# Twelve input projection groups per layer as seven products of quarters, with the mix kept in DRAM, in a two-layer hybrid decoder trunk

## The chip, the cores and the metric

One NeuronCore of one Trainium2 chip runs the whole program. The metric is the device time of one execution in microseconds (us); lower is better. A core has TensorE (PE; its weight loads are PEld), VectorE (DVE), ScalarE (ACT), GpSimd (POOL) and SyncE (SP), which here only issues DMAs. Each works through its own instructions in the order in which the program was built.

## What is computed

Two layers. Each normalises its input, multiplies it by one wide input matrix, runs three head groups on the product (short convolution, stick-breaking attention, gated linear attention or GLA), multiplies each by a SiLU gate, and sends the 2048 mixed columns through an output matrix into the residual stream. Cut to what matters:

```python
D_MODEL = 2048; SEQ = 512; DEPTH = 2
h = _rmsnorm(x, norm_g)
proj = h @ w_in                         # 512 x 2048 times 2048 x 7696
(cv_h, cv_b, cv_c, cv_g, sb_q, sb_k, sb_v, sb_g, gl_q, gl_k, gl_v, gl_g, gl_lr) = split(proj)
y_conv = cv_b * (conv3(cv_c * cv_h) + conv_b) * silu(cv_g)                 # 512 columns
y_sb   = stick_breaking(rms(sb_q), rms(sb_k), sb_v) * silu(sb_g)           # 8 heads of 128
g      = log_sigmoid(gl_lr @ gla_w_up + gla_b_up) / 16
y_gla  = rms(gla(gl_q, gl_k, gl_v, g)) * silu(gl_g)                        # 4 heads, 512 columns
x      = x + concat([y_conv, y_sb, y_gla]) @ w_out
```

## The kernel before

Everything is float32 at the interface. Each factor of a large product is held as two float16 parts, high and low, and a product is three matmuls: high by high, high by low, low by high.

**Groups.** The columns of both matrices are worked off in groups of 256 (`specs`, lines 301 to 316): per layer 30 groups of `w_in` in the order gla v 0, v 1 (with 16 more columns, `gl_lr`), q, k, gate 0, gate 1, conv h, c, g, b of the first half, then four times (j = 0 to 3) v, g, q, k of two attention heads, then conv h, c, g, b of the second half; then 8 groups of `w_out`. A group is a step of a pipeline. `fetch(i+2)` (line 332) issues two DMAs of 1 MB on SP's queue into one of two `st` buffers. `load(i+1)` (line 423) makes the float16 parts: ACT squares and sums both halves for a bound (`wmax`, line 352), POOL sums over the partitions (line 362), DVE makes a scale (lines 363 to 379), ACT writes the high halves (`whi`, line 415, 128x2048 each) and DVE the low halves (`wlo`, line 421). The parts go into three pairs of buffers `wh`, `wl`, of which a plain group uses two. The call to `weights()` (line 467) at the start of group i starts `fetch(i+2)` and `load(i+1)` with a higher priority than the rest.

**Products on PE.** `project_cols` (line 611) makes 96 matmuls of 512 moving columns (lines 623 to 625), the result transposed; `project_toks` (line 635) and `project_by_token` (line 730) make 192 of 256 (lines 631 to 633, and 738). `project_quick` (line 686) forms the product from seven products of quarters instead of eight, and is used for the output groups in `QUICK` (line 30): three in layer 0 and four in layer 1. It makes 336 matmuls of 128 columns (line 698). It needs sums of quarters of both factors. Those of the weights are made in `wsums` (line 436): four DVE additions in place on the `st` buffer (lines 456, 458, 459, 462) and seven splits of 128x1024, each one ACT copy (line 450) and one DVE subtraction (line 451). They fill all three `wh`, `wl` pairs and a fourth pair, taken from `e` and `ga`. Those of the mix are made in `msums` (line 648), once a layer: 24 DVE operations (line 655) and 8 ACT copies (line 665), all 128x1024. Between the products ACT and DVE read the two PSUM banks of the group (lines 709 to 727), and a product that writes a bank waits for the reader of that bank (product 3 for the ACT copy at line 709, product 4 for the DVE subtraction at line 711).

**Around them.** GLA is in lines 912 to 1028: for each of two pairs of heads, seven levels of DVE, ACT and PE work, then a normalisation. It is emitted after the GLA gates, and its instructions lie beside the groups conv h 0 to v 0. Its float16 scratch (`src16`, `tgt16`, `att16`, lines 770 to 776) lies in the part of the mix buffers that the attention heads fill later. The attention of pair j (lines 1104 to 1165) is cut in four pieces that run beside the groups of the next pair (`go`, line 1100). For q and k of a pair the product is copied out of PSUM (line 1198), normalised in a chain of small DVE operations (line 1205 and lines 1207 to 1214), split (lines 1218, 1219) and transposed by DMA.

**The mix** is two SBUF tensors `mh`, `ml` of 128x4x16x128 float16. `mixsplit` (line 787) writes one block of 128 columns of it, on ACT and DVE; `weight_ratio` (line 1030) brings all blocks to one scale before the output groups.

**Order of the work.** The first 50 us or so of ACT and DVE are written out by hand (lines 553 to 604). Everything else is put into each engine's order by a scheduler when the program is built, by priority and by its own estimate of when an instruction is ready; at run time each engine keeps that order.

Of the kernel before, what the change touches and what calls it, by code (L numbers as in the profile page):

```python
# [17 lines left out]
P = 128  # L18
EPS = 1e-6
TAU = 16.0  # L20
XBITS = 8.0
# [8 lines left out]
QUICK = ((3, 4, 6), (3, 4, 5, 6))  # L30

AHEAD = (8, 17, 21)


# [5 lines left out]
def hybrid_trunk(ctx, tc, x, norm_g, w_in, conv_w, conv_b, sb_qn_g, sb_kn_g,  # L40
# [16 lines left out]
    big = ctx.enter_context(tc.tile_pool(name="big", bufs=4))  # L57
# [13 lines left out]
    def sm(n, tag, bufs=None):  # L71
        return small.tile([P, n], F32, tag=tag, name=nm(tag), bufs=bufs)
# [4 lines left out]
    def newbig(tag, shape, dt):  # L77
        return big.tile(shape, dt, tag="big", name=nm(tag))
# [12 lines left out]
    xt = [newbig("x", [P, 2, D], F32) for _ in range(2)]  # L91
# [210 lines left out]
    specs = []  # L302
    for l in range(depth):
        for cols in ([(GL_V, GW)], [(GL_V + GW, GW), (GL_LR, LR)], [(GL_Q, GW)], [(GL_K, GW)],
                     [(GL_G, GW)], [(GL_G + GW, GW)]):
            specs.append((l, w_in, cols))
        conv = [[(l, w_in, [(c0 + j * GW, GW)]) for c0 in (CV_H, CV_C, CV_G, CV_B)] for j in range(2)]
        specs += conv[0]
        for j in range(4):
            for c0 in (SB_V, SB_G, SB_Q, SB_K):  # L310
                specs.append((l, w_in, [(c0 + j * GW, GW)]))
        specs += conv[1]
        for gi in range(NG):
            if gi in QUICK[l]:
                quick.add(len(specs))
            specs.append((l, w_out, [(gi * GW, GW)]))
# [8 lines left out]
    staged, whole, peak, scales = {}, {}, {}, {}  # L325
# [6 lines left out]
    def fetch(i):  # L332

        l, src, cols = specs[i]
        staged[i] = st = []
        whole[i] = stage.tile([P, KT, GX], F32, tag="st", name=nm("st"))
        for h in range(2):
            s_ = whole[i][:, h * HK:(h + 1) * HK, :]
            o = 0
            for c0, w in cols:  # L340
                nc.sync.dma_start(
                    s_[:, :, o:o + w],
                    src[l, h * HK * P:(h + 1) * HK * P, c0:c0 + w].rearrange("(k p) n -> p k n", p=P))
                o += w
            st.append(s_)

    def wmax(i, h):

        n = sum(c[1] for c in specs[i][2])
        if h == 0:  # L350
            peak[i] = sm(2, "wm")
        S.activation(junk(HK * n).rearrange("p (k n) -> p k n", k=HK), staged[i][h][:, :, :n], AF.Square,  # L352
                     accum_out=peak[i][:, h:h + 1])

    def wscale(i):
# [4 lines left out]
        if i:  # L360
            gm = sm(2, "wgm")
            G.partition_all_reduce(gm, peak.pop(i), P, RED.add)  # L362
            V.tensor_scalar(m, gm[:, 0:1], gm[:, 1:2], 2.0 ** -120, ALU.add, ALU.max)  # L363
# [47 lines left out]
    def whi(i, h):  # L411
        n = sum(c[1] for c in specs[i][2])
        wh = wpool.tile([P, HK, GX], F16, tag="wh", name=nm("wh"))
        wl = wpool.tile([P, HK, GX], F16, tag="wl", name=nm("wl"))
        lasthi[i] = S.activation(wh[:, :, :n], staged[i][h][:, :, :n], AF.Copy, scale=scales[i])  # L415
        loaded[i][0].append((wh, wl))

    def wlo(i, h):
        n = sum(c[1] for c in specs[i][2])
        wh, wl = loaded[i][0][h]  # L420
        V.scalar_tensor_tensor(wl[:, :, :n], staged[i][h][:, :, :n], scales[i], wh[:, :, :n], ALU.mult, ALU.subtract)  # L421
# [14 lines left out]
    def wsums(i):  # L436
# [7 lines left out]
        parts.append([wk([P, HK * P], t, dt=F16) for t in ("e", "ga")])  # L444
# [99 lines left out]
    def halves(tag):  # L544

        return [newbig(tag, [P, NT, KT, P], F16) for _ in range(2)]

    mix = halves("x")
# [58 lines left out]
    for l in range(depth):  # L607
# [40 lines left out]
        def msums():  # L648

            parts = [[wk([P, 2, HK, P], tag, bufs, F16) for _ in range(2)] for tag, bufs in  # L650
                     (("zw", None), ("v", None), ("th", 2))]
            parts.append([wk([P, 2, HK, P], tag, 1, F16) for tag in ("raw", "qp")])
# [4 lines left out]
            if last:  # L657
                room = [a[:, n] for a in [newbig("x", [P, 4, HK, P], F32) for _ in range(2)] for n in range(3)]
            for t in range(2):
                (h11, h12), (h21, h22), (l11, l12), (l21, l22) = (  # L660
                    (a[:, q, 0::2, :], a[:, q, 1::2, :]) for a in mix for q in (t, t + 2))
# [6 lines left out]
                if last:  # L668
                    e, g, f = room[3 * t:3 * t + 3]
                else:  # L670
                    e, g, f = (wk([P, HK, P], tag) for tag in ("g", "g", "kT"))
# [14 lines left out]
        def project_quick(sums):  # L686
# [4 lines left out]
            a11, a12, a22 = ([a[:, 2 * r:2 * r + 2, c::2, :] for a in mix] for r, c in ((0, 0), (0, 1), (1, 1)))  # L691
            s_, a21_22, a12_s, a11_21 = sums

            def prod(o, w, a, start, stop=False):
                for t in range(2):
                    for kk in range(HK):
                        for i, (p_, q_) in enumerate(((0, 0), (0, 1), (1, 0))):
                            T.matmul(o[:, t * P:(t + 1) * P], a[p_][:, t, kk, :], w[q_][:, kk, :],  # L698
                                     start=start and t == kk == i == 0, stop=stop and kk == HK - 1 and i == 2,
                                     skip_group_check=True)  # L700

            def half(a, r, c):
                return y[:, 2 * r:2 * r + 2, c * P:(c + 1) * P], a.rearrange("p (t c) -> p t c", c=P)

            y = wk([P, NT, GW], "g")
            tmp = wk([P, 4, GW], "g")
            p1, v_, d7, u_ = (tmp[:, n, :] for n in range(4))
# [8 lines left out]
            o, a = half(pa, 0, 0)  # L716
            S.activation(o, a, AF.Copy)
            prod(pb, wt1, a21_22, False, True)
            V.tensor_tensor(u_, pb, p1, ALU.subtract)
            o, a = half(pf, 0, 1)  # L720
            V.tensor_tensor(o, a, half(u_, 0, 1)[1], ALU.add)
            o, a = half(u_, 1, 1)
            V.tensor_tensor(o, a, half(d7, 1, 1)[1], ALU.subtract)
            yield 0, y[:, :2, :].rearrange("p a c -> p (a c)"), u
            prod(pd, wT4, a22, False, True)
            o, a = half(pd, 1, 0)
            V.tensor_tensor(o, a, half(v_, 1, 0)[1], ALU.subtract)
            yield 2, y[:, 2:, :].rearrange("p a c -> p (a c)"), u
# [14 lines left out]
        def gate(ps, u, mx=None, logistic=False):  # L743

            g = wk([P, 2, seq], "g")
            for c in range(2):
                y = g[:, c, :]
                if logistic:
                    tables.append(S.activation(y, ps[c], AF.Sigmoid, scale=u))
                    for a in tables[-9:-1]:  # L750
                        order(tables[-1], a)
                    V.scalar_tensor_tensor(y, ps[c], u, y, ALU.mult, ALU.mult)
# [9 lines left out]
            if mx is not None:  # L762
                V.tensor_reduce(mx, g, AX.XY, ALU.max, apply_absolute_value=True)
            return g

        mix = halves("m")
        mh, ml = mix


        spare = [[mh[:, t, 4:12, :].rearrange("p k c -> p (k c)")[:, n * seq:(n + 1) * seq] for n in range(2)]  # L770
                 for t in range(NT)]
# [539 lines left out]
```

## Time and profile before

| what | value |
|---|---|
| time, median of three runs | 1719.39 us (1718.61 to 1720.03) |
| time of the profiled execution | 1721.89 us |
| span of that execution, first instruction to last | 1720.1 us |
| granted TensorE clock, mean | 0.997 |
| HBM read, written | 173.36 MB, 8.39 MB |

Times within the trace count from the start of the span. A row of the groups view has the source line, the engine, the operation, what it writes and reads, the shape, the count, the busy time, the mean length of one in ns, and the idle time of the engine before it with what ended it. A row of the windows view has for each engine the busy time in that stretch and the instruction count, then the granted clock and the busy share of the DMA engines.

### The profile page before, as it was taken

What the parts mean: (1) busy time and instruction counts of PE and PEld (TensorE: products, weight loads), DVE (VectorE), ACT (ScalarE), POOL (GpSimd) and SP (SyncE); (2) the same over time, 40 slices, a digit from 0 to 9 for tenths busy, and PEclk for the clock granted to TensorE, in tenths of its full rate; (3) what the DMA queues carried; (4) which work ended last, traced back from release to release, by engine and by line L of the source; (5) the groups of instructions that cost most, each with busy time, mean ns of one, the idle gap of its engine ahead of it and who ended that gap; (6) DMA issues with size and microseconds to landing.
All of it is one profiled execution on the core that took longest, in us unless ns stands there. A gap on an engine that the chain in (4) does not pass through costs nothing. (4 is left out here: it accounts for less than half of the span.)

```text
span 1720.1 us, 32415 instructions
## 1 busy us (share of the span) xinstructions
PE 1702.0 (99%) x13770; PEld 1227.2 (71%) x13770; DVE 1166.7 (68%) x2149; ACT 1022.4 (59%) x1243; POOL 63.5 (4%) x104
## 2 busy tenths in 40 slices
PE   7999999999999999999999999999999999999998
PEld 5744557878787764799986454668686868548998
DVE  8566897566666656786675588974656566567883
ACT  7558676555555555566655575864555555545661
POOL 1100000000000000000010000000000000000000
PEclk9999999999999999999999999999999999999999
DMA  7323321344444445145544231223544433343441
GB/s 251 98 98 98 99 98 54 113 120 126 119 121 123 129 123 153 61 156 181 181 116 148 83 108 55 99 98 111 126 127 126 125 108 108 116 137 123 148 155 45
DMA packets 266641, 204.95 MB, mean 119 GB/s; under 512 B 93362, under 2 KB 265724, under 8 KB 265984
## 3 DMA queue, kind: packets, MB, share of 16 engines
q1 hardware_dynamic: 257488, 193.42, 37.1%
q10 hardware_dynamic: 9008, 9.45, 1.6%
q8 instruction: 108, 1.77, 0.4%
q14 instruction: 37, 0.30, 0.1%
HBM read 173.36 MB, written 8.39 MB: 106 GB/s over the span
## 5 line engine op out<-in xcount | busy, mean ns | idle before, releaser
L421 DVE SCALAR_TENSOR_TENSOR wl<-st,ws,wh 128x2048 f16<-128x2048 f32 (+1 forms) x138 | 324.4, 2352 | 205.3 <-ACT wh L415 205.3
L415 ACT ACTIVATE wh<-st,ws 128x2048 f16<-128x2048 f32 (+1 forms) x136 | 272.0, 2003 | 247.0 <-PE psp L633 111.0
L633 PE MATMUL psp<-wh,m 128*128 128x256 f16 x1216 | 331.5, 273 | 0.0
L632 PE MATMUL psp<-wl,m 128*128 128x256 f16 x1216 | 331.4, 273 | 0.0
L631 PE MATMUL psp<-wh,m 128*128 128x256 f16 x1216 | 331.4, 273 | 0.0
L352 ACT ACTIVATE junk<-st 128x2048 uint8<-128x2048 f32 (+1 forms) x150 | 285.5, 1903 | 4.9 <-DMA st<-in_w_out_dram 3.0
L633 PE MATMUL psp<-wh,x 128*128 128x256 f16 x768 | 209.3, 273 | 0.0
L632 PE MATMUL psp<-wl,x 128*128 128x256 f16 x768 | 209.3, 273 | 0.0
L631 PE MATMUL psp<-wh,x 128*128 128x256 f16 x768 | 209.3, 273 | 0.0
L623 PE MATMUL psp<-m,wh 128*128 128x512 f16 x512 | 194.0, 379 | 0.0
L624 PE MATMUL psp<-x,wh 128*128 128x512 f16 x512 | 194.0, 379 | 0.0
L624 PE MATMUL psp<-m,wh 128*128 128x512 f16 x512 | 194.0, 379 | 0.0
L623 PE MATMUL psp<-x,wh 128*128 128x512 f16 x512 | 194.0, 379 | 0.0
L625 PE MATMUL psp<-x,wl 128*128 128x512 f16 x512 | 193.9, 379 | 0.0
L625 PE MATMUL psp<-m,wl 128*128 128x512 f16 x512 | 193.9, 379 | 0.0
L625 PEld LDWEIGHTS <-wl 128*128 128x128 f16 x1024 | 100.2, 98 | 119.7
L624 PEld LDWEIGHTS <-wh 128*128 128x128 f16 x1024 | 100.2, 98 | 118.7 <-issue 2.6
L623 PEld LDWEIGHTS <-wh 128*128 128x128 f16 x1024 | 100.2, 98 | 117.5 <-issue 1.9
L631 PEld LDWEIGHTS <-m 128*128 128x128 f16 x1216 | 119.0, 98 | 13.9
L633 PEld LDWEIGHTS <-m 128*128 128x128 f16 x1216 | 119.0, 98 | 13.9
L632 PEld LDWEIGHTS <-m 128*128 128x128 f16 x1216 | 119.0, 98 | 13.8
L363 DVE TENSOR_SCALAR wq<-wgm 128x1 f32<-128x1 f32 x75 | 15.9, 212 | 111.1 <-POOL wgm L362 111.1
(356 smaller groups left out, 2665.0 us busy)
## 6 DMA issues: line engine op xcount, KB each, us to landing
st<-in_w_in_dram SPq DMA_DIRECT2D x120, 1024.0 KB, 7.7
st<-in_w_out_dram SPq DMA_DIRECT2D x32, 1024.0 KB, 7.6
x<-in_x_dram SPq DMA_DIRECT2D x4, 1024.0 KB, 5.1
qT<-in_x_dram ACTq DMA_DIRECT2D x8, 512.0 KB, 6.4
qT<-xs ACTq DMA_DIRECT2D x8, 512.0 KB, 3.9
xs<-x SPq DMA_DIRECT2D x14, 256.0 KB, 3.8
out_dram<-kT SPq DMA_DIRECT2D x14, 256.0 KB, 2.1
th<-za SPq DMA_TRANSPOSE x64, 3.1
```

Source lines behind the costliest of these rows:

```text
L352: S.activation(junk(HK * n).rearrange("p (k n) -> p k n", k=HK), staged[i][h][:, :, :n], AF.Square, accum_out=peak[i][:, h:h + 1])
L363: V.tensor_scalar(m, gm[:, 0:1], gm[:, 1:2], 2.0 ** -120, ALU.add, ALU.max)
L415: lasthi[i] = S.activation(wh[:, :, :n], staged[i][h][:, :, :n], AF.Copy, scale=scales[i])
L421: V.scalar_tensor_tensor(wl[:, :, :n], staged[i][h][:, :, :n], scales[i], wh[:, :, :n], ALU.mult, ALU.subtract)
L623: T.matmul(o, wh[:, kk, cs], xh[:, :, k, :], start=st_, stop=False)
L624: T.matmul(o, wh[:, kk, cs], xl[:, :, k, :], start=False, stop=False)
L625: T.matmul(o, wl[:, kk, cs], xh[:, :, k, :], start=False, stop=en)
L631: T.matmul(o, ah[:, t, k, :], wh[:, kk, :n], start=st_, stop=False, skip_group_check=True)
L632: T.matmul(o, ah[:, t, k, :], wl[:, kk, :n], start=False, stop=False, skip_group_check=True)
L633: T.matmul(o, al[:, t, k, :], wh[:, kk, :n], start=False, stop=en, skip_group_check=True)
```

## The change

- Twelve `w_in` groups of each layer (`QUICK_IN`) go through `project_quick`: both GLA gates, conv h, c, g of the first half, v of pairs 1 and 3, g of all four pairs, and conv h of the second half. All but the two v groups give a transposed result; there `project_quick` makes 168 matmuls of 256 columns, for the v groups 336 of 128.
- The sums of quarters of the input are made once a layer (`xsums`), after the decay of GLA is known in the program's text, by the code that makes those of the mix.
- The result of a quick group is put together in an SBUF tile of its own (`dst`) that is taken when the group starts; a plain group is still read from PSUM.
- The large buffers stay four of 128x16 KB, but two on each of two sides. The sums of the input lie where the mix was. So `mixsplit` writes to a `ga` tile and a DMA on SP's queue stores it in DRAM (`mixd`); after conv h of the second half `mixload` reads what is there back in six DMAs, and the last four blocks are written to SBUF as before.
- The scratch of GLA lies in the attention buffers `qp` and `th`.
- The `st` buffer is 256 columns wide; the 16 columns of `gl_lr` have a tile and a DMA of their own. The fourth pair of weight buffers has tiles of its own. Most small tiles have one buffer in place of two. One power of two in the scale of x changes.

The parts of the diff that the text speaks of:

```diff
+QUICK_IN = ("gla gate 0", "gla gate 1", "conv h 0", "conv c 0", "conv g 0", "v 1", "g 0", "g 1", "g 2", "v 3", "g 3",
+            "conv h 1")
...
-        parts.append([wk([P, HK * P], t, dt=F16) for t in ("e", "ga")])
+        parts.append([wk([P, HK * P], t, 1, dt=F16) for t in ("w7h", "w7l")])
...
+        def xsums():
+
+            parts = []
+            for _ in range(2):
+                a = newbig("s", [P, 4, 2, HK, P], F16, 1 - l)
+                parts.extend([a[:, 2 * n], a[:, 2 * n + 1]] for n in range(2))
+            return sums_of((xh, xl), parts, lambda t: [wk([P, HK, P], tag) for tag in ("zw", "zw", "g")])
...
-        def project_quick(sums):
+        def project_quick(src, sums, y, cols):
...
+                            if cols:
+                                T.matmul(o, w[q_][:, kk, :], a[p_][:, :, kk, :], start=st_, stop=en,
+                                         skip_group_check=True)
+                            else:
+                                T.matmul(o[:, t * P:(t + 1) * P], a[p_][:, t, kk, :], w[q_][:, kk, :], start=st_,
+                                         stop=en, skip_group_check=True)
...
             prod(pa, w11, a11, True)
-            S.activation(p1, pa, AF.Copy)
+            S.activation(y12, za, AF.Copy)
             prod(pb, wT2, s_, True)
-            V.tensor_tensor(v_, pb, p1, ALU.subtract)
+            V.tensor_tensor(y21, zb, y12, ALU.subtract)
             prod(pd, wT3, a11_21, False)
-            S.activation(d7, pd, AF.Copy)
+            S.activation(y22, zd, AF.Copy)
             prod(pf, w22, a12_s, False)
             prod(pa, w21, a12, False)
...
+        def project(cols, dst):
+
+            if cursor[0] not in quick:
+                return project_cols() if cols else project_toks(xh, xl)
+            y = dst()
+            for _, u in project_quick((xh, xl), insums, y, cols):
+                pass
...
-            S.activation(mh[:, ts_, k, :], y3, AF.Copy, scale=s_)
-            V.scalar_tensor_tensor(ml[:, ts_, k, :], y3, s_, mh[:, ts_, k, :], ALU.mult, ALU.subtract)
+            if mix:
+                hi, lo = (a[:, :, k, :] for a in mix)
+            else:
+                hl = wk([P, 2, NT, P], "ga", dt=F16)
+                hi, lo = hl[:, 0], hl[:, 1]
+            S.activation(hi, y3, AF.Copy, scale=s_)
+            V.scalar_tensor_tensor(lo, y3, s_, hi, ALU.mult, ALU.subtract)
+            if not mix:
+                nc.sync.dma_start(mixd[l][:, :, k, :], hl.rearrange("p i t c -> p (i t) c"))
+
+        def mixload():
+
+            mix.extend(halves("m", 1 - l))
+            for ks in (slice(0, 2), slice(4, 10), slice(12, KT)):
+                assert all(k in split for k in range(ks.start, ks.stop))
+                for i in range(2):
+                    nc.sync.dma_start(mix[i][:, :, ks, :], mixd[l][:, i * NT:(i + 1) * NT, ks, :])
...
+        insums = xsums()
+        scr = [wk([P, 2, 2, seq], *a, F16) for a in (("qp", 1), ("th", 2), ("th", 2))]
...
         for j in range(4):
             bm = sm(2, "bm")
-            ps, u = project_toks(xh, xl)
+            ps, u = project(False, lambda: wk([P, NT, GW], "kT"))
```

More of the change, by code (lines that the diff above doesn't have):

```diff
@@ L20 @@
 TAU = 16.0
-XBITS = 8.0
+XBITS = 7.0
 RED = bass_isa.ReduceOp
@@ L90, in hybrid_trunk @@
     xs = dram.tile([seq, D], F32, tag="xs", name="xs")
-    xt = [newbig("x", [P, 2, D], F32) for _ in range(2)]
+    xt = [newbig("x", [P, 2, D], F32, 1) for _ in range(2)]
     def xload(t):
@@ L666, in put @@
                     do(V.tensor_tensor, lo, a, hi, ALU.subtract)
[L668 to L671, printed above, removed]
+                e, g, f = room(t)
                 do(V.tensor_tensor, f, h22, l22, ALU.add)
@@ L706, in project_quick @@
-            tmp = wk([P, 4, GW], "g")
-            p1, v_, d7, u_ = (tmp[:, n, :] for n in range(4))
+                            st_ = start and t == kk == i == 0
+                            en = stop and kk == HK - 1 and i == 2
+                            if cols:
[4 more added lines that the diff above has]
+                                         stop=en, skip_group_check=True)
@@ L748, in gate @@
                 if logistic:
[L749 to L752, printed above, removed]
+                    a = wk([P, seq], "ga") if quick_ else y
+                    tables.append(S.activation(a, ps[c], AF.Sigmoid, scale=u))
+                    for b in tables[-9:-1]:
+                        order(tables[-1], b)
+                    V.scalar_tensor_tensor(y, ps[c], u, a, ALU.mult, ALU.mult)
                     continue
```

209 lines of the change are left out of this document (117 added, 92 removed).

## The prediction

> **What bounds the kernel now.** I read first the page's sums and slices, then the windows around the GLA stage, then the groups, last the timeline at the places where PE waits.
>
> ```profile
> span 1720.1 us, 32415 instructions
> ...
> PE 1702.0 (99%) x13770; PEld 1227.2 (71%) x13770; DVE 1166.7 (68%) x2149; ACT 1022.4 (59%) x1243; POOL 63.5 (4%) x104
> ...
> DVE  8566897566666656786675588974656566567883
> ```
>
> PE is busy 99% of the span, so over the whole program PE sets the time and fewer matmul cycles should shorten it. DVE is at 68%, but the slices (43 us each) are uneven: with the first layer's GLA (slices 4 to 6) and the second's (24 to 26) it reaches 8 and 9 tenths. So I read those stretches alone; in the windows view the columns after the length are PE, PEld, DVE, ACT, POOL, granted clock, DMA share, GB/s.
>
> ```profile
> 53.30:273.80 220.50, 220.50 (x1350) 122.35 (x1349) 164.49 (x358) 148.06 (x218) 5.07 (x12) 1.00 0.29 96
> 226.30:273.80 47.50, 47.50 (x362) 31.01 (x361) 45.97 (x100) 39.01 (x72) 0.85 (x2) 1.00 0.27 90
> 158.70:283.20 124.50, 124.50 (x863) 74.24 (x861) 109.71 (x221) 88.62 (x151) 2.26 (x5) 1.00 0.26 86
> 902.30:1122.40 220.10, 220.10 (x1346) 121.94 (x1345) 162.12 (x341) 148.17 (x218) 5.05 (x12) 1.00 0.29 96
> ```
>
> The first and the last row run from the end of the load of gla v 1 to the end of the load of g 0, in either layer. These ends come from the timeline (start, length, then the operation):
>
> ```profile
> 50.85 2.48 DVE L421 SCALAR_TENSOR_TENSOR wl<-st,ws,wh 128x2176 f16<-128x2176 f32 x1 [1.51 <-ACT wh L415]
> ...
> 271.51 2.33 DVE L421 SCALAR_TENSOR_TENSOR wl<-st,ws,wh 128x2048 f16<-128x2048 f32 x1
> ...
> 283.22 0.38 PE L623 MATMUL psp<-x,wh 128*128 128x512 f16 x1
> ...
> 305.66 0.27 PE L631 MATMUL psp<-wh,x 128*128 128x256 f16 x1
> ...
> 899.84 2.48 DVE L421 SCALAR_TENSOR_TENSOR wl<-st,ws,wh 128x2176 f16<-128x2176 f32 x1 [3.92 <-ACT wh L415]
> ...
> 1120.07 2.34 DVE L421 SCALAR_TENSOR_TENSOR wl<-st,ws,wh 128x2048 f16<-128x2048 f32 x1
> ...
> 1154.21 0.27 PE L631 MATMUL psp<-wh,m 128*128 128x256 f16 x1
> ```
>
> The load of g 0 is done at 273.8, PE starts g 0 at 283.22 and ends it at 305.66, where q 0 starts. So the weights are ready 32 us before the group's end. That lead hides everything DVE does here, and it is all there is: in the stretch DVE has only 220.5 - 164.5 = 56 us idle. In the second layer the group ends at 1154.21.
>
> **What PE saves.** The spacing of matmuls is taken where nothing else runs:
>
> ```profile
> 96.00:115.00 19.00, 19.00 (x89) 8.62 (x88) 11.19 (x24) 11.82 (x15) 0.53 (x2) 1.00 0.04 10
> ...
> 1684.66 10.88 PE psp L698 x192
> ...
> 1695.54 20.97 PE psp L738 x192
> ```
>
> 512 columns take 19.00 / 88 = 0.216 us (x89 counts one cut by the edge), 256 take 20.97 / 192 = 0.109, 128 take 10.88 / 192 = 0.0567 at the end of the program and a little less in longer runs; I use 0.056. A plain group is 96 x 0.216 = 20.7 or 192 x 0.109 = 21.0. A quick group with a transposed result is 168 x 0.109 = 18.35, which saves 2.4; one of the v groups is 336 x 0.056 = 18.8, which saves 2.2. Twenty of the one and four of the other: 56 us, if nothing else came to bound. All costs below are set against this.
>
> **What DVE gets.**
>
> ```profile
> L421 DVE SCALAR_TENSOR_TENSOR wl<-st,ws,wh 128x2048 f16<-128x2048 f32 (+1 forms) x138 | 324.4, 2352 | 205.3 <-ACT wh L415 205.3
> ...
> L451 DVE SCALAR_TENSOR_TENSOR wl<-st,ws,wh 128x1024 f16<-128x1024 f32 x42 | 53.1, 1279 | 7.7 <-ACT wh L450 7.7
> ...
> L450 ACT ACTIVATE wh<-st,ws 128x1024 f16<-128x1024 f32 x42 | 46.4, 1141 | 23.4 <-PE psp L698 9.7 <-DVE st L458 6.0 <-PE psp L633 3.0
> ...
> L456 DVE TENSOR_TENSOR st<-st 128x1024 f32<-128x1024 f32 x7 | 8.6, 1224 | 0.2
> ...
> L655 DVE TENSOR_TENSOR g<-m,g 128x1024 f32<-128x1024 f16 x4 | 4.9, 1221 | 0.0
> ...
> L719 DVE TENSOR_TENSOR g<-psp,g 128x256 f32<-128x256 f32 x7 | 3.0, 422 | 2.7 <-PE psp L698 2.7
> ```
>
> - A plain load costs DVE two subtractions, 2 x 2.35 = 4.7 us. A quick one costs seven of 1.28 and four additions of 1.22, 13.85: 9.1 more.
> - The five DVE steps between the products cost 5 x 0.42 = 2.1 a group; before, a plain group has none of these.
> - The sums of x are 24 operations of 1.22, 29.3 a layer. They are taken as the rows of the mix show, both with float32 and with float16 inputs.
>
> By loads of 24 groups this is 24 x 11.2 + 2 x 29.3 = 328 us, so DVE would go to about 1495, some 85% of the span: an average that fits. The stretch does not. Six of its loads are quick (both gates, conv h, c, g, and g 0), five quick groups are read out within it, and all sums stand ahead of the first gate in the built order: 6 x 9.1 + 5 x 2.1 + 29.3 = 94.4, against 56 idle. Rows that follow each other closely overlap a little:
>
> ```profile
> 1657.00 1.28 DVE wl L451
> ...
> 1658.68 1.19 DVE wl L451
> 1659.87 1.13 DVE st L462
> ```
>
> The step from the second to the third is 1.19 where the group's mean is 1.28; on about 100 added operations at 0.08 this takes off 8, so 86 to 94. The end of g 0 is then where DVE's work puts it: 53.3 + 164.5 + (86 to 94) + one last product of 24 matmuls, 2.6 = 306 to 315, and idle time of DVE has to be added. Second layer: 902.3 + 162.1 + (86 to 94) + 2.6 = 1153 to 1161.
>
> That idle time, r, is what no row shows directly. DVE waits for ACT's half of each split, for the scale, and for PE where it reads PSUM. From below: the densest 47.5 us of the same stretch have 1.53 idle, 3.2%, which on some 254 us of work is 8. From above: the 124.5 us with 109.71 busy have 11.9% idle, 34. But these 11.9% were idle with PE ahead, when DVE had no work due, so I go near the dense row and take 5%, 13 us. With the middle of the two sums, layer 0 ends g 0 at 310.5 + 13 = 323.5 against 305.7: **+18**. Layer 1: 1157 + 13 = 1170 against 1154.2: **+16**. In this the five groups' saving on PE is gone, since PE waits for weights. PE alone would need 252.4 - 6 x 2.4 = 238 from 53.3 to the end of g 0; DVE needs some 268.
>
> ACT gets 7 x 1.14 for 2 x 2.0 a load, two copies and eight copies for the sums, some 40 us on 148 in the stretch: below DVE, so not the bound, though it makes part of r.
>
> **What follows the stretch.** Four transposed groups (g 1, g 2, g 3, conv h 1) and two v groups a layer keep their saving: 4 x 2.4 + 2 x 2.2 = 14, twice, **-28**. Here DVE has room:
>
> ```profile
> 306.00:707.00 401.00, 401.00 (x3018) 292.18 (x3016) 247.37 (x464) 223.93 (x229) 10.82 (x21) 1.00 0.41 117
> ```
>
> Idle are 154 us, added are 6 x 11.2 = 67. That hides the sum but not every wait. A product that writes a PSUM bank waits for its reader, and the two v groups come right behind k of the pair before, whose normalisation stands on DVE and ACT:
>
> ```profile
> 347.58 0.27 PE L631 MATMUL psp<-wh,x 128*128 128x256 f16 x1
> ...
> 355.35 2.19 DVE L1214 SCALAR_TENSOR_TENSOR raw<-raw,qr,kg 128x128 f32<-128x128 f32 x8
> ...
> 357.57 1.06 ACT L1218 ACTIVATE qp<-raw 128x1024 f16<-128x1024 f32 x1 [6.64 <-DVE raw L1214]
> ```
>
> k 0 ends and v 1 starts at 347.58; the ACT copy of k starts at 357.57, 10.0 later, because DVE's chain ends there. In the built order the copy of v 1's first product stands on ACT behind this copy of k, and v 1's product 3 needs the bank. Ahead of the chain DVE now has one split and two additions, 1.28 + 2.44, for one subtraction of 2.35: +1.4. So the bank is free at 10.0 + 1.06 + 1.4 + 0.4 = 12.9 after k's end. PE has two products of v 1 (5.4) and the first of g 1 (2.6) to do, 8.0, and then waits 4.9. Queued behind that product on PE are all the rest of v 1 and g 1, so the 4.9 is on the path. From below it is nothing, if DVE does the chain earlier; the row nearest to it is this chain, so I take 4.9. After such a wait the clock is low:
>
> ```profile
> 884.47 1.05 PE L738 MATMUL psp<-wh,m 128*128 128x256 f16 x8 [2.82 <-DMA m<-raw]
> ...
> 884.50:888.00 3.50, 3.50 (x21) 3.06 (x22) 2.20 (x4) 1.76 (x2) 0.00 (x0) 0.63 0.19 54
> 888.00:892.00 4.00, 4.00 (x35) 3.48 (x33) 2.86 (x2) 0.23 (x1) 0.00 (x0) 0.89 0.01 4
> ```
>
> A gap of 2.82 us was followed by a granted clock of 0.63 and 0.89: 3.5 x 0.37 + 4 x 0.11 = 1.7 lost. With it 6.6 for each of v 1 and v 3 in two layers: **+26**.
>
> **What is hidden.** The mix blocks go to DRAM and back, 3 MB each way a layer, on SP's queue.
>
> ```profile
> st<-in_w_in_dram SPq DMA_DIRECT2D x120, 1024.0 KB, 7.7
> ...
> SPq L341 <- DVE wl L421: 471.0, 48, 26.9
> ```
>
> At 7.7 us a MB the six reloads take some 24 us of the queue, and three groups, 60 us, lie between conv h 1 and the first output group. The stores are queued ahead of fetches on SP, and those fetches stand waiting for the `st` buffer anyway (471 us in 48 waits). I cost both at nothing; without that cover one fetch behind one store is some 8 us late. GLA's scratch in the attention buffers is idle space at that time: nothing. Single buffers of small tiles add waits of the order of one small operation, below 0.5 us each, off the path but part of r. The `st` buffer 16 columns narrower changes two DMAs: nothing.
>
> **The sum.** +18 + 16 - 28 + 26 = +32 on the profiled execution, 1721.9 (its span 1720.1 and 1.8 around it), which is 1754. The median of the runs shown is 2.5 below that execution: **1752 us**.
>
> **Rivals.**
> 1. DVE's queue stays full: its sums and splits are many short pieces with nothing to wait for, and GLA's steps fill the holes. Then r is 3% or less and the sums are the lower ones: 306.4 + 8 - 305.7 = +9 and 1153 + 8 - 1154.2 = +7, no waits at v 1 and v 3, -28: -12, **1707**; with r at zero 1691. It speaks for it that the densest window really is at 97%; against it, that a bank wait needs only one copy out of place. It decides the sign where r of both layers and the four waits together fall below some 18 us.
> 2. DVE's queue is as loose as in the 124 us row, since splits go back and forth with ACT: r = 34 in each layer, 42 more: **1794**.
> 3. The clock. PE now has gaps within the stretch, and after gaps the clock was 0.63. PE needs 238 us at full clock against 268 on DVE, so it decides below a mean of 0.89; at 0.80 PE needs 297, +29 a layer: **1810**. Against it: most gaps would be short and spread, where the one before 884.47 was 2.82 us. The Trainium skill, TensorE: Matmul & The Clock Gate, section "What's actually happening", says that the clock falls to half only after an idle window of about 3.4 us, and comes back after as long a time of work. By that page gaps under 3.4 us would cost no clock, so this rival would fall away and the forecast stay as it is; the trace disagrees with it, since 0.63 follows 2.82 us of waiting, and the measurement decides.
> 4. The queue of SP: weights fetched late behind mix stores in the attention stage. Such a load stood on the chain near the end of the program:
>
> ```profile
> 1644.84 9.00 DMA st<-in_w_out_dram
> ```
>
> Three such in a layer would be 2 x 3 x 9 = +54, **1806**. Against it: the 471 us of waiting for buffers.
>
> **How the numbers follow.** The forecast's mechanism gets 0.50, with times from 1722 (four waits of nothing) to 1776; rival 1 gets 0.20 (1691 to 1718), rival 2 0.18, rivals 3 and 4 0.06 each. The range goes from 1702 to 1794: it leaves out about 0.07 below (r near zero) and 0.12 above. A difference of 0.2%, 3.4 us, is about what measurements of this kernel can tell from none. Faster: rival 1 but for its upper end, and a rest, 0.20. Same: the seam between it and the forecast, 0.08. Slower: 0.72.
>
> **What would show it.** Right, if the changed profile has PE idle behind DVE's splits from the gates to g 0 in both layers, DVE over 93% in that stretch, g 0 ending near 323 and 1170 less or plus what comes before, the granted clock below 1 there, and PE waiting at v 1 and v 3 for the ACT copy. Rival 1: no PE wait at v 1, g 0 ending within 10 us of before. Rival 2: DVE under 90% with PE idle. Rival 4: waits for a DMA of `st` on PE's path before the output groups. My forecast is wrong in its base if the GLA work of DVE moves behind the load of g 0, which frees the stretch, or if most of the sums of x lie ahead of it.

## The result and the profile after

The changed kernel takes 1814.72 us (median of four runs, 1811.98 to 1817.08) against 1719.71 for the kernel before. The ratio is 1.0551, with a 95% interval from 1.0531 to 1.0572. The forecast was 1752 with a range to 1794. The sign is right. The size is not: +95 us in place of +32. In what follows, a time with a ratio is a median of several executions, and one without is a single execution; executions of one kernel lay up to some 6 us apart. Line numbers are those of the changed kernel, or of the run's own kernel, which differ by a few lines.

The page of the changed kernel, its sums and two of its slices (DVE, and the granted TensorE clock in tenths):

```profile
span 1810.9 us, 37130 instructions
...
PE 1687.5 (93%) x15786; PEld 1384.3 (76%) x15786; DVE 1447.8 (80%) x2539; ACT 1149.2 (63%) x1459; POOL 75.7 (4%) x106
...
DVE  8989997768687786777598899976687868767884
PEclk9998989999999999999999999999999999999999
```

PE falls from 99% to 93%. The time is in the places where PE now waits, and DVE's 80% is an average again. Windows around the same stages show where (columns as in the prediction):

```profile
53.30:344.90 291.60, 253.22 (x1994) 188.65 (x1994) 262.04 (x502) 199.51 (x294) 17.05 (x18) 0.94 0.27 86
...
344.90:754.60 409.70, 394.89 (x3601) 326.25 (x3600) 306.22 (x555) 253.85 (x284) 11.86 (x22) 0.98 0.47 131
947.30:1238.00 290.70, 251.72 (x1984) 186.51 (x1982) 257.69 (x475) 199.78 (x293) 14.34 (x16) 0.95 0.27 86
```

The first row runs from 53.3 us, where the prediction's stretch starts, to the end of g 0 in the first layer. That took 252.4 us before and takes 291.6. PE is busy for 253.2 of them at a mean clock of 0.94, and 253.2 x 0.94 = 238: just the need of PE that the prediction named. So the stretch is 238 of work, some 38 of gaps and some 15 of low clock.

From PE's rows the end of each group can be set against its end in the kernel before. The difference grows like this (us, plus is later):

| at the end of | layer 0 | layer 1 |
|---|---|---|
| gla k (start of the stage) | +3.0 | +45.2 |
| conv c 0 | +16.9 | +60.3 |
| conv b 0 | +31.9 | +75.1 |
| g 0 | +39.3 | +83.8 |
| q 1 (behind v 1, g 1) | +45.7 | +89.2 |
| q 2 (behind g 2) | +43.4 | +86.8 |
| q 3 (behind v 3, g 3) | +49.6 | +91.9 |
| the last output group | +47.4 | +90.9 |

Four losses repeat in both layers (PE runs conv g 0 and conv b 0 interleaved, so they are one step): some 14 us up to conv c 0 (15 in the second layer), 15 from there to conv b 0, 7 to 9 to g 0, and 5 to 6 net at each of the pairs v 1, g 1 and v 3, g 3. What releases PE in its longest waits, over the whole program (waits for, total, times, longest):

```profile
PE psp L735 <- ACT kT L743: 13.6, 4, 4.4
PE psp L732 <- ACT wh L471: 13.1, 7, 4.4
PE psp L645 <- ACT wh L432: 11.9, 2, 9.8
PE psp L732 <- DVE v L1242: 11.5, 2, 5.8
PE psp L732 <- DVE wl L472: 8.4, 7, 2.7
```

The first line is the wait that the prediction names at v 1 and v 3. The second, third and fifth are weights that come late. The fourth stands between v 0 and g 0, and nothing in the prediction speaks of it.

### The profile page after: what moved, and what is told of

Same layout as the page of the kernel before. It is cut to its first block, busy times and chain, and to the rows that moved or that the text cites. A ratio compares the mean times of both kernels' runs of the same rounds, so it can differ in the third digit from the quotient of the medians.

```text
span 1810.9 us, 37130 instructions
## 1 busy us (share of the span) xinstructions
PE 1687.5 (93%) x15786; PEld 1384.3 (76%) x15786; DVE 1447.8 (80%) x2539; ACT 1149.2 (63%) x1459; POOL 75.7 (4%) x106
## 5 line engine op out<-in xcount | busy, mean ns | idle before, releaser
L653 PE MATMUL psp<-wh,m 128*128 128x256 f16 x1088 | 296.4, 273 | 2.9 <-DVE v L1242 1.8
L655 PE MATMUL psp<-wh,m 128*128 128x256 f16 x1088 | 296.5, 273 | 0.0
L472 DVE SCALAR_TENSOR_TENSOR wl<-st,ws,wh 128x1024 f16<-128x1024 f32 x186 | 235.0, 1279 | 71.4 <-ACT wh L471 71.1
L365 ACT ACTIVATE junk<-st 128x2048 uint8<-128x2048 f32 x150 | 285.0, 1900 | 4.4 <-DMA st<-in_w_out_dram 2.9
L471 ACT ACTIVATE wh<-st,ws 128x1024 f16<-128x1024 f32 x186 | 205.8, 1140 | 88.6 <-PE psp L655 33.5
L732 PE MATMUL psp<-s,wh 128*128 128x256 f16 x1280 | 229.8, 280 | 27.5 <-ACT wh L471 8.2
L439 DVE SCALAR_TENSOR_TENSOR wl<-st,ws,wh 128x2048 f16<-128x2048 f32 x90 | 211.1, 2348 | 54.2 <-ACT wh L432 53.6
L432 ACT ACTIVATE wh<-st,ws 128x2048 f16<-128x2048 f32 x88 | 175.5, 1998 | 93.3 <-DVE wp L395 31.2
L732 PEld LDWEIGHTS <-wh 128*128 128x128 f16 x1920 | 193.2, 101 | 47.4 <-ACT wh L471 15.5
L732 PE MATMUL psp<-s,wl 128*128 128x256 f16 x640 | 178.8, 280 | 4.9 <-DVE wl L472 4.3
L653 PE MATMUL psp<-wh,x 128*128 128x256 f16 x640 | 174.3, 273 | 2.9 <-DVE v L1242 1.9
L655 PE MATMUL psp<-wh,x 128*128 128x256 f16 x640 | 174.4, 273 | 0.0
L645 PE MATMUL psp<-x,wh 128*128 128x512 f16 x192 | 74.0, 385 | 9.8 <-ACT wh L432 9.8
```

The lines of the kernel that those rows point to most:

```text
L365: S.activation(junk(HK * GW).rearrange("p (k n) -> p k n", k=HK), staged[i][h], AF.Square, accum_out=peak[i][:, h:h + 1])
L432: lasthi[i] = S.activation(wh[:, :, :GW], staged[i][h], AF.Copy, scale=scales[i])
L439: V.scalar_tensor_tensor(wl[:, :, :GW], staged[i][h], scales[i], wh[:, :, :GW], ALU.mult, ALU.subtract)
L471: hi = S.activation(h_, b, AF.Copy, scale=sc)
L472: V.scalar_tensor_tensor(l_, b, sc, h_, ALU.mult, ALU.subtract)
L645: T.matmul(o, wh[:, kk, cs], xh[:, :, k, :], start=st_, stop=False)
```

## The experiments

The theory at the start: the quick groups' work on DVE makes the loss. Against it stood the moves that came with them (mix through DRAM, scratch, single buffers).

**e1. No quick input group at all**, the sums left out, all moves kept.

```diff
-QUICK_IN = ("gla gate 0", ...)
+QUICK_IN = ()
-        insums = xsums()
+        insums = None
```

> All twelve input groups plain again and the sums of the input left out; the mix still goes through DRAM, GLA scratch still lies in the attention buffers, the small tiles are still single, the st buffer is 256 wide. Theory (the time comes from the quick groups' work on DVE and the waits it makes): 1712 to 1730 us, PE without gaps in the GLA stage. Rival (the moves of the mix and the scratch and the single buffers cost the time): 1760 us or more.

Measured: 1746.36 us, ratio 1.0164 (1.0147 to 1.0181). Both expectations miss: the moves alone cost some 28 us (the kernel before took 1718.58 beside it). The groups' ends show where: +10.4 and +10.3 us between the end of v 0 and that of g 0, once a layer, and little elsewhere. The timeline of e1 there (ACT first, then PE and DVE):

```profile
295.06 0.72 ACT L838 ACTIVATE ga<-za,gsmix 128x512 f16<-128x512 f32 x1 [3.50 <-DVE za L1090]
295.69 0.61 ACT L805 ACTIVATE ga<-g 128x512 f32<-128x512 f32 x1
...
299.20 0.63 ACT L805 ACTIVATE ga<-g 128x512 f32<-128x512 f32 x1 [0.19 <-DMA mixd<-ga]
```
```profile
305.38 0.59 PE L644 MATMUL psp<-x,wh 128*128 128x512 f16 x1 [7.79 <-DVE g L801]
```
```profile
306.49 1.41 DVE L1153 SCALAR_TENSOR_TENSOR kT<-psp,wu,kT 128x512 f32<-128x512 f32 x2
```

L838 writes GLA's last mix block into a `ga` buffer, on its way to DRAM. L805 is conv's gate, which takes `ga` too. Buffers of a name go round in the order of the program's text, and there GLA stands ahead of conv's gate. So the gate waits for the last GLA block, and once for its store. Without the gate the product of conv b 0 cannot be used: it is read from PSUM only at 306.5 (L1153). Until then it keeps two of the three banks, v 0 and g 0 share the third, and PE stands 7.8 us for its reader.

**e2. v 1 and v 3 plain.**

```diff
-            ... "v 1", "g 0", "g 1", "g 2", "v 3", "g 3",
+            ... "g 0", "g 1", "g 2", "g 3",
```

> v 1 and v 3 plain, the other ten quick. In the trace of the changed kernel the two pairs v 1, g 1 and v 3, g 3 lose 5.1 to 6.4 us net each time, 23.1 in all, which with the 18.4 us that these eight groups save is 41.5 of waits. Theory (the wait is that of v's product 3 for a copy behind k's normalisation): the waits go with v 1 and v 3, of the savings 8.8 go too, so about 33 us less than the changed kernel: 1778 to 1787 us. Rival (g 1 and g 3 are late with their weights whatever v does): 1805 us or more.

Measured: 1787.03 us, 27.7 less than the changed kernel. The waits go with the v groups. With the 8.8 us of savings that go too, the four waits are worth 36.5, 9.1 each. By the groups' ends they are worth 10.3 each, and some 7 us of that are lost again elsewhere.

**e3. Only g 1, g 2, g 3 and conv h 1 quick.** (`QUICK_IN` cut to these four.)

> Only g 1, g 2, g 3 and conv h 1 are quick; the sums of the input are made at their place ahead of the GLA gates. Theory: the sums, 29 us of DVE a layer, fit into the 56 us that DVE has idle in the GLA stage, and eight groups save 2.4 us each: 1696 to 1708 us, faster than before. Rival (any work added to DVE in the GLA stage comes out in the time): 1730 us or more.

Measured: 1731.58 us, ratio 1.0072 (1.0057 to 1.0087). The theory misses, and the time lies within the rival's bound (1730 or more). The rival's reason does not hold, though: with the sums made, it is still 14.8 us less than e1, of the 19.2 that eight groups save, so the sums cost little. The wait of e1 is in it, and e6 takes that away.

**e4. Only the five groups of the GLA stage quick.** (`QUICK_IN` cut to both gates and conv h, c, g of the first half.)

> Only the five groups of the GLA stage ahead of conv b 0 are quick (both gates, conv h, c, g); sums of the input as in the changed kernel. The stage of the changed kernel lost 39.3 and 38.8 us against before. Theory (DVE's work in that stage makes it): most of it stays, 25 to 38 us a layer, so 1770 to 1795 us. Rival (the loss of the stage needs the quick g 0 behind it): 1745 us or less.

Measured: 1804.15 us. g 0 ends at +39.1, as with all twelve. The loss of the stage does not need the quick g 0, and it is larger than the expectation had it.

**e5 and e6. Buffers of their own for the mix blocks**, on e1 and on e3.

```diff
-                hl = wk([P, 2, NT, P], "ga", dt=F16)
+                hl = wk([P, 2, NT, P], "mx", dt=F16)
...
-        parts.append([wk([P, HK * P], t, 1, dt=F16) for t in ("w7h", "w7l")])
+        parts.append([wk([P, HK * P], t, dt=F16) for t in ("e", "ga")])
```

> As e1 (no quick input group, no sums of the input), but the blocks of the mix on their way to DRAM get two buffers of their own in place of the two ga buffers, and the fourth pair of weight parts goes back to e and ga as before. Theory: in e1 the gate of conv takes ga behind the last GLA blocks, so conv b 0 keeps two of three PSUM banks to 307 us and v 0 and g 0 share one; that stall of 10.4 and 10.3 us goes: 1720 to 1730 us. Rival (the gate of conv is late with DVE's GLA work, whatever buffer it takes): 1740 us or more.

> As e3 (g 1, g 2, g 3 and conv h 1 quick, sums of the input made), with the buffers of e5. Theory: e3 less the stall between v 0 and g 0, 10.9 and 10.8 us there, about 1710 us (1705 to 1716), faster than before. Rival: 1726 us or more.

Measured: e5 1724.15 us, ratio 1.0026 (1.0016 to 1.0035); e6 1705.96 us, ratio 0.9916 (0.9900 to 0.9933). In e5 g 0 ends at +1.6 in place of +11.6. So the shared `ga` made the wait, and all other moves together, the way through DRAM among them, cost 4 to 5 us. e6 is 0.8% faster than the kernel before. Its page:

```profile
span 1704.3 us, 33904 instructions
...
PE 1682.0 (99%) x14346; PEld 1282.1 (75%) x14346; DVE 1289.2 (76%) x2315; ACT 1076.0 (63%) x1331; POOL 78.1 (5%) x106
```

PE is at 99% again, with 20 us less to do, while DVE does 122 us more than before.

**e7. The sums of the input left out.** Four quarters of the input stand in for the sums, so the products are not those of the reference.

```diff
-        insums = xsums()
+        insums = [[a[:, 2 * r:2 * r + 2, c::2, :] for a in (xh, xl)] for r, c in ((0, 0), (0, 1), (1, 0), (1, 1))]
```

> The changed kernel, but the sums of quarters of the input are left out: four quarters of the input stand in for them. That takes 29 us off DVE ahead of the first gate in each layer. Theory (up to conv b 0 the queue of DVE sets the time): 20 to 29 us less a layer, 1757 to 1775 us. Rival (the sums fill time that DVE has, and the cost is the chain of splits of each group): 1798 us or more.

Measured: 1813.63 us, so nothing is gained. The theory falls as it stood: 29 us a layer less work on DVE ahead of the first gate changes the time by 1 us, which is within what executions differ by.

**e8. The additions of quarters of the weights left out**, for input groups; the splits take single quarters, so the products are others.

```diff
+        def add(o, a, b):
+            if specs[i][1] is w_out:
+                V.tensor_tensor(o, a, b, ALU.add)
...
-        V.tensor_tensor(b11, b11, b12, ALU.add)
+        add(b11, b11, b12)
```

> The changed kernel, but the four additions of quarters of the weights are left out in the loads of input groups, whose seven splits take single quarters; the output groups are as they were. That takes 4.9 us off DVE a quick load, some 25 a layer up to g 0, and the waits of splits for additions. Theory (queue of DVE): 18 to 28 us less a layer, 1758 to 1780 us. Rival (PSUM readers and GLA's own chain set the stage): 1798 us or more.

Measured: 1772.17 us, 42.6 less. conv c 0 ends at +7.5 in place of +16.9, conv b 0 at +16.0 in place of +31.9. So the additions count, and the sums do not. Of the 20.8 us that the first layer gains, half come at the pairs v 1, g 1 and v 3, g 3 (+2.1 and +0.6 net in place of +6.4 and +6.2). e8 takes two things at once: 4.9 us of DVE work in each quick load, and the waits of splits for the additions. It does not tell them apart.

The window from the loads of the second gate to those of conv b 0 shows where each stands; in order the changed kernel, e7 and e8:

```profile
120.00:230.00 110.00, 95.10 (x850) 80.78 (x848) 105.50 (x188) 84.67 (x132) 4.09 (x4) 0.94 0.24 78
```
```profile
120.00:230.00 110.00, 92.45 (x829) 78.28 (x828) 106.11 (x189) 84.05 (x133) 3.27 (x4) 0.94 0.25 80
...
53.30:230.00 176.70, 157.97 (x1231) 117.36 (x1229) 149.80 (x311) 121.45 (x176) 7.95 (x12) 0.96 0.26 86
```
```profile
120.00:230.00 110.00, 96.49 (x873) 81.28 (x871) 94.42 (x188) 86.36 (x137) 2.95 (x6) 0.94 0.29 94
```

DVE is busy for 105.5 and 106.1 of 110 us, 96%, with the sums or without them. They stand ahead of 120 us, where DVE has room: in e7 it is busy there for 149.8 - 106.1 = 43.7 of 66.7 us. For the additions of four loads it is the window itself.

**e9. A second set of weight parts.** As e7, and every second quick input group takes its parts from the space that the sums left.

```diff
+        second[0] += specs[i][1] is w_in
+        other = specs[i][1] is w_in and second[0] % 2 == 0
+        if other:
+            a = [newbig("w", [P, 7, HK * P], F16, 1 - specs[i][0]) for _ in range(2)]
+            parts.extend([p_[:, n, :] for p_ in a] for n in range(7))
```

> As e7 (sums of the input left out, quarters of the input stand in), and every second quick input group takes its fourteen weight parts from the space of the sums, so that a quick group and the next one share no buffer. Theory (a quick group fills all weight buffers, so the load of the next one waits for the products of this one and loses its lead): at least half of the 36 to 39 us a layer that the GLA stage loses goes, and part of the waits at v 1 and v 3: 1735 to 1778 us, against 1813.6 of e7. Rival (splits wait in the queues of DVE and ACT behind GLA's steps, with any number of buffers): 1798 us or more.

Measured: 1822.06 us. The weight buffers as the cause fall: conv h 0 ends at +2.4 (e7: +16.5), but conv c 0 at +12.4 (+12.9) and conv b 0 at +29.6 (+28.1).

**e10 and e11. Mix blocks in the fourth pair of weight buffers**, with all twelve groups, and with seven (gla gate 0, conv h 0, conv g 0 and the four of e6).

```diff
-                hl = wk([P, 2, NT, P], "ga", dt=F16)
+                hl = wk([P, 2, NT, P], ("w7h", "w7l")[k % 2], 1, dt=F16)
```

> The changed kernel, but the blocks of the mix on their way to DRAM lie in the fourth pair of weight buffers in place of ga. Theory: the wait between v 0 and g 0 (7.6 us of gaps and some 4 us of low clock in the first layer) goes, 7 to 11 us a layer: 1793 to 1802 us. Rival: the readers of conv b 0 are as late for want of DVE, 1809 us or more.

> Seven quick groups: g 1, g 2, g 3 and conv h 1 as in e6, and gla gate 0, conv h 0 and conv g 0, each of which has plain groups on both sides; mix blocks as in e10. Theory (the buffers): a plain neighbour leaves buffers free, so each of the three costs little or saves up to 2.4 us, 1693 to 1712 us. Rival (any quick load in the GLA stage costs there what the five of e4 do, some 6 us each and more): 1735 us or more.

Measured: 1873.48 and 1806.14 us (e11: ratio 1.0509, 1.0492 to 1.0527). Both lie beyond their rivals' bounds, but not for the rivals' reasons: both made a new wait of the kind that they were to remove. The load of conv g 0 in e10:

```profile
291.56 1.15 ACT L471 ACTIVATE w7h<-st,ws 128x1024 f16<-128x1024 f32 x1 [1.81 <-DMA mixd<-w7h]
```

Its last part stands behind GLA's mix blocks in the round of `w7h`, so conv g 0 ends 83 us later than before (e11: 80). What they tell about their questions is little. In e11 conv c 0 ends at -3.6, 6.6 less than at the start of the stage. Two quick groups save 4.8, so some of PE's other work has moved behind it.

**e12. conv g 0 plain.** The other eleven stay quick. The reason is a coincidence in all runs so far: the copy of conv g 0's first product (L743, which writes its `g` buffer) starts right behind the end of GLA's first pair (L1091, which reads the `g` buffers of GLA's gates).

```profile
245.06 0.74 DVE L1091 SCALAR_TENSOR_TENSOR za<-za,par,g 128x512 f32<-128x512 f32 x1
```
```profile
246.46 0.36 ACT L743 ACTIVATE g<-psp 128x256 f32<-128x256 f32 x1
```

> The changed kernel with conv g 0 plain, eleven groups quick. In every run with conv g 0 quick the copy of its first product starts 1.3 to 1.5 us after the second multiplication of GLA's first pair by its gate (246.5 after 245.1, 242.8 after 241.4, 239.8 after 238.4): its result takes a g buffer, and both are held by the GLA gates until then. Theory (that buffer makes the step from +16.9 at conv c 0 to +31.9 at conv b 0): plain, the product waits in PSUM, conv b 0 ends at +14 to +22, 10 to 18 us less a layer: 1779 to 1796 us. Rival (the step is the work of DVE in four quick loads one behind the other): 1805 us or more.

Measured: 1796.07 us, at the upper edge of the expectation. conv b 0 ends at +18.3 in place of +31.9, as expected; of the 13.6 us some 6 are lost again up to g 0, where the wait for `ga` is still there.

**e13. Own places for both.** As e7, with conv g 0's result and the six mix blocks of GLA and conv in the space of the sums.

```diff
+                own = mx is None and not logistic
-                g.append(wk([P, 2, seq], "g"))
+                g.append(newbig("r", [P, 2, seq], F32, 1 - l) if own else wk([P, 2, seq], "g"))
...
+                if k in (12, 13, 14, 15, 0, 1):
+                    if not blocks:
+                        blocks.append(newbig("b", [P, 6, 2, NT, P], F16, 1 - l))
+                    hl = blocks[0][:, (12, 13, 14, 15, 0, 1).index(k)]
```

> As e7 (sums of the input left out, quarters stand in), and in the space of the sums lie the result of conv g 0 and the six blocks of the mix from GLA and conv, in place of g and ga. Theory (the two buffers that wait for the end of GLA make most of the stage's loss): against e7, 18 to 26 us less a layer, 1760 to 1779 us. Rival (GLA itself ends late and everything with it): 1797 us or more.

Measured: 1772.16 us, 41.5 less than e7. conv b 0 ends at +13.9 (e7: +28.1), g 0 at +15.8 (+35.6). The copy no longer waits for GLA; these are the same two instructions in e13:

```profile
227.62 0.36 ACT L743 ACTIVATE r<-psp 128x256 f32<-128x256 f32 x1
```
```profile
241.20 0.73 DVE L1097 SCALAR_TENSOR_TENSOR za<-za,par,g 128x512 f32<-128x512 f32 x1
```

**e14. Six quick groups** (gla gate 0, conv h 0 and the four of e6), mix blocks as in e10.

> Six quick groups: the four of e6, and gla gate 0 and conv h 0, which stand apart from each other and from conv g 0; mix blocks in the fourth pair of weight buffers, which no load wants between conv h 0 and g 1. Theory (a quick group that stands alone saves its 2.4 us in the GLA stage too): e6 less 5 to 10 us, 1694 to 1702 us. Rival (a quick load costs DVE more than the stage has): 1712 us or more.

Measured: 1712.76 us, ratio 0.9947 (0.9927 to 0.9967): faster than before, slower than e6, beyond the rival's bound by 0.8. In the first layer g 0 ends 3 us ahead of e6. In the second it loses more than that between v 0 and q 0, where PE waits again for a reader of PSUM. Whether a quick group that stands alone pays in that stage stays open.

**e15 and e16.** e9 with conv g 0 plain, and e13 with v 1 and v 3 plain (one or two names fewer in `QUICK_IN`; sums left out as in e7).

> e9 and e12 together: sums of the input left out, a second set of weight parts for every second quick input group, conv g 0 plain. In e9 conv h 0 ended only 2.4 us later than before in place of 16.5 (e7), and all came back at conv g 0, which waits for its g buffer. Theory (the weight buffers make the loss up to conv c 0, the g buffer hides that they do): with conv g 0 plain the gain of the second set stays; conv b 0 ends at 0 to +8 in the first layer, and the time is 1745 to 1776 us. Rival (density of DVE's work, with any buffers): conv b 0 at +15 or later, 1788 us or more.

> e13 with v 1 and v 3 plain. If the waits at v 1 and v 3 and those for g and ga are separate, the 27 to 33 us of e2 come off the 1772.2 of e13: 1737 to 1746 us. If they share a cause, 1755 us or more.

Measured: 1817.11 and 1735.69 us. In e15 conv b 0 ends at +16.5, where the rival had it: more weight buffers don't help, with or without the wait for `g`. In e16 36.5 us come off e13, a little over the expectation. So the waits for `g` and `ga` and those at the v groups add up.

```profile
span 1733.9 us, 35800 instructions
...
PE 1665.2 (96%) x15210; PEld 1367.9 (79%) x15210; DVE 1352.5 (78%) x2435; ACT 1113.3 (64%) x1411; POOL 81.7 (5%) x106
```

PE is back at 96%. What is left in e16 is mostly the 12 us that each layer loses up to conv c 0.

## Why the prediction was wrong in size

**What PE saves** was right. At g 2, where nothing else happens, the table falls by 2.3 and 2.4 us. From the end of q 3 to that of the second conv b, with conv h 1 the only quick group between, the difference falls by 2.4 and 1.7, and in e2, without the waits, g 1 and g 3 save 2.2 to 2.4 each. The 238 us of PE's work in the stage came out. The 2.2 of a v group is not shown alone, since its wait covers it.

**The waits at v 1 and v 3** were right in mechanism and place, too small in size: 4.9 plus 1.7 was forecast, 9 to 10 is measured (e2). The changed kernel at v 1, on ACT:

```profile
397.66 0.38 ACT L743 ACTIVATE g<-psp 128x256 f32<-128x256 f32 x1 [4.10 <-PE psp L732]
400.60 1.06 ACT L1289 ACTIVATE qp<-raw 128x1024 f16<-128x1024 f32 x1 [2.56 <-DVE raw L1285]
401.56 0.36 ACT L743 ACTIVATE kT<-psp 128x256 f32<-128x256 f32 x1
```

v 1's copy (the last row) does stand behind the copy of k. It ends 15.1 us after the start of v 1 at 386.85, not 12.9. PE waits 4.4 us there, some 2.3 more ahead of it for weights of g 1, and runs at low clock afterwards.

**The stretch, "+18" and "+16", is the step that failed**: +36.3 and +38.6 between the ends of gla k and g 0. It took g 0 to end 2.6 us behind its load on DVE, at 323.5. In the changed kernel these rows stand at g 0 (its first product, and the last split of its load):

```profile
322.32 0.37 PE L732 MATMUL psp<-x,wh 128*128 128x256 f16 x1 [5.77 <-DVE v L1242]
```
```profile
328.39 1.29 DVE L472 SCALAR_TENSOR_TENSOR w7l<-st,ws,w7h 128x1024 f16<-128x1024 f32 x1 [0.61 <-ACT w7h L471]
```

The load ends at 329.7, 8.8 us behind the forecast's 320.9, and g 0 at 345.1, another 15.4 behind it: what held its end was not its load but its late start, behind the reader of v 0's product. The step has three errors.
- The idle time of DVE was taken as one sum, 56 us. In the kernel before it lies in two places, 26.8 us ahead of 120 and 28.4 from there to 230:

```profile
53.30:120.00 66.70, 66.70 (x396) 38.49 (x395) 39.89 (x110) 36.70 (x41) 2.42 (x6) 1.00 0.38 124
120.00:230.00 110.00, 110.00 (x612) 54.52 (x611) 81.61 (x162) 76.02 (x112) 2.20 (x5) 1.00 0.26 86
```

  The sums of x all lie in the first: 8.5 us of them even ahead of 53.3, 20.3 from there to 120, none behind. e7 shows 1 us for them in place of some 29 a layer.
- From 120 to 230 us DVE is at 96%, close to the 95% that r = 5% means, and e8 gets 9.4 of the 13.9 us up to conv c 0 back. So work of DVE in the loads costs time there, but that its amount is the bound is not shown: e8 shortens the chain of each load too, and behind 230 us DVE is as full, 54.41 of 56.90 us in the row below, while e13 takes 14 us off at that place with buffers alone.

```profile
230.00:286.90 56.90, 44.87 (x336) 29.03 (x334) 54.41 (x111) 38.32 (x66) 1.40 (x2) 0.88 0.29 89
```

- The rest, 20 us a layer, is two buffers of small names, `g` and `ga` (e13 against e7). "Single buffers of small tiles ... off the path" had looked at how many buffers there are, not at who takes them. A quick group takes its result's buffer when it starts, a plain one waits in PSUM; conv g 0 so waits for GLA's gates. Mix blocks take `ga` where before they were written in place; conv's gate so waits for GLA's end.

**The clock**, rival 3, was held to matter only in place of DVE's bound. It adds to it: some 15 us of the first layer's stretch, by the windows above. It follows the gaps: in e6, where PE is busy for 251.5 of the 252.3 us from 53.3 on, the clock is 1.00.

**The signs** that the prediction named came out in part. PE waits at v 1 and v 3 for the ACT copy, and the clock in the stretch is below 1. DVE is not over 93% there: by the windows at the top it is busy for 262.0 of 291.6 us and for 257.7 of 290.7, 90% and 89%. That is next to rival 2 (under 90%, 1794 us), but not for its reason: in the first layer's stretch DVE's splits of quick loads wait 4.5 us in all for ACT. DVE is at 90% ahead of 120 us, at 96% from there to 286.9 and at 73% behind that. The nearest number is rival 3's 1810, by chance: its mean clock of 0.80 is 0.94 here. Rival 4's sign is absent: among PE's waits stands none for a DMA of `st`.

**What was hidden** was rightly held to be so for the way of the mix through DRAM and for SP's queue: e5 has all of it and costs 4.7 us.

**The sum**, against the 1721.9 of the profiled execution before and the 1812.7 of the profiled one after: 29 us for the part up to conv c 0 of both layers, 30 from there to conv b 0, 16 to g 0, 23 net for the pairs, -9 for g 2 and conv h 1 of both layers, and 2 for the rest (+3.0 ahead of the first stage, -2.2 ahead of the second, +0.7 at the end) make 91.

What stays open: how the 14 us up to conv c 0 divide between DVE's total, the chain of splits and additions in a load, and the order in which these and GLA's steps stand, since each edit also makes the scheduler write another order.

## What to carry to other kernels

When a change moves an intermediate from PSUM, or from its final place, into a shared buffer, list for that buffer's name all takers in the order of the program's text and ask when the one ahead lets go. A taker late in time and early in the text holds up all behind it, and no share of busy time shows that: two stretches with DVE at 96% lost time here, and in the second it was a buffer. Idle time of an engine is worth counting by the stretch in which it lies: ahead of 120 us DVE without the sums was a third idle, and 29 us of work there cost next to nothing.

## What the runs showed of the hardware

The clock after a long wait. Behind the 9.79 us gap of PE in the changed kernel, and behind the wait at v 1:

```profile
241.93 0.61 PE L645 MATMUL psp<-x,wh 128*128 128x512 f16 x1 [9.79 <-ACT wh L432]
...
401.98 0.26 PE L735 MATMUL psp<-wh,s 128*128 128x128 f16 x1 [4.36 <-ACT kT L743]
```
```profile
402.00:410.00 8.00, 8.00 (x97) 8.00 (x97) 1.25 (x2) 0.38 (x1) 0.00 (x0) 0.66 0.29 66
242.00:250.00 8.00, 5.77 (x14) 1.83 (x15) 7.94 (x17) 4.33 (x10) 0.00 (x0) 0.50 0.45 141
...
400.70:407.40 6.70, 5.42 (x52) 5.42 (x52) 1.56 (x2) 1.33 (x3) 0.00 (x0) 0.50 0.35 78
407.60:410.00 2.40, 2.40 (x46) 2.40 (x44) 0.00 (x0) 0.08 (x1) 0.00 (x0) 1.00 0.00 0
```

The clock was 0.50 for the whole 8 us after 242 (a second gap of 2.23 us lies in them), and 0.66 in the 8 us after a gap of 4.36, which is 2.7 us lost against the 1.7 that the prediction took from the start of layer 1. The Trainium skill, TensorE: Matmul & The Clock Gate, section "What's actually happening", gives half the clock after an idle window and full clock after about 3.4 us of sustained work. The 0.50 agrees with it. At v 1 PE works again from 401.98 on and the clock is 0.50 up to 407.4: 5.4 us at half clock, longer than its 3.4, and the measurement decides.
